# A block of gated linear attention, gated DeltaNet and MLP: the turned keys stored in whole rows, their 32x32 blocks put in place by GpSimd's loads

## The chip, the cores and the metric

The kernel runs on one core of a Trainium2 chip. The metric is the device time of one execution in microseconds (us). Runs of one kernel are summed up by their median; a profiled execution gives, besides its own time, a trace of every instruction and transfer. Engine names are short in the profile: PE is TensorE's matmul, PEld its weight load, DVE is VectorE, ACT is ScalarE, POOL is GpSimd, and SP is the engine that does nothing here but issue transfers. "SPq", "ACTq" and "POOLq" are the issues of transfers from these engines.

## What is computed

One layer over 1024 tokens of width 1024. After a norm with a modulation from a conditioning vector, one wide projection `w_in` gives the inputs of two branches: gated linear attention (GLA, 4 heads) and a gated delta rule (GDN, 8 heads). Their outputs are merged under sigmoid gates, projected by `w_out` and added to the input; a squared-ReLU MLP follows. The part that the change touches is the gated delta rule, cut here to what matters:

```python
k = l2_norm(silu(causal_short_conv(h @ w_in[keys])))        # 8 heads of 128 channels
def step(state, inp):                                        # over the chunks of 64 tokens
    qd, at, uu, ww, ks, dc = inp
    v_new = uu - einsum('bhcd,bhdv->bhcv', ww, state)
    o = einsum('bhcd,bhdv->bhcv', qd, state) + einsum('bhij,bhjv->bhiv', at, v_new)
    state = dc[..., None, None] * state + einsum('bhcd,bhcv->bhdv', ks, v_new)
```

The last product, keys times new values, sums over tokens, so it needs the keys with the token on the partitions. The projection leaves them the other way, with the channel on the partitions.

## The kernel before

All matmuls are float32 split into a high and a low half, three products each, on tiles of 128 x 512. The kernel is written as one stream of dense tiles. `dense_b` (line 477) makes one tile of 128 output channels by 1024 tokens in 8 steps, and each step ends in `tick()` (line 384). All other work is put on an agenda in ticks with `at` (line 373) and is emitted between the dense matmuls when its tick comes. `next_w` (line 472) fetches and casts the weights of the tile after the next: a block of 256 columns is loaded by SP into one of two buffers `raw`, ACT casts it to the high half `wH`, DVE subtracts for the low half `wL`.

The order on an engine is set by `InOrder` (from line 28). While it is strict, each instruction of that engine is issued after the one emitted before it. It is strict for PE, DVE, ACT, POOL and the queue `DMA` (SP) from the start until the second tile of `branch_gate` (lines 139 and 1507 to 1510). In the GDN heads it is strict again for PE, DVE and ACT only, and for POOL and SP from head 7 on (line 1870); until then the build orders POOL's and SP's queues as it expects their items to become ready. `ST` (line 68) is ACT's queue without `InOrder`.

Three stages matter here.

*Key phase.* The key tiles of the 8 heads are made one after another. `key_head` (line 749) schedules the rest of a head: the keys are stored as they are (`kT_d`), DVE turns them in 32x32 blocks into `kb` (`turn`), ACT squares `kb`, PE makes the Gram products, DVE multiplies them with the decays (`times`, line 786), and `spill` stores the result (`X_d`, `a21_d`). `V.transpose` turns each 32x32 block in its place, so each block is turned but the blocks stand where they were: the block of channels c and tokens (t, b) lies in row group c at columns (t, b), and has to come to row group b, columns (t, c). In the kernel before this is done on the way out: `spread` (lines 759 to 763) issues four stores, one for each 32 partitions of `kb`, in pieces of 32 floats (128 bytes), 1024 pieces a store, so that `kt_d[h]` holds the keys in their final order.

*Gates.* `branch_gate` (line 1392) makes 8 tiles with the `C_MA` columns of `w_in`. ACT applies tanh to a tile (`sig`) and stores it through `ST` to `sg_d`, 4 ticks later (line 1396).

*GDN heads.* `gdn_head` (line 919) runs 24 ticks of dense tiles for each head. At line 1025 one load brings `kt_d[h]` into `ktok`, a tile of the pool `hd` with 4 buffers, two of them in each head; PE uses it from tick 26 on (`c2`, line 1066). Heads 0 to 4 finish late: 62 ticks after their start POOL stores a row of norms (`on_d`, in `roots`), at tick 66 it loads that row broadcast to all partitions (`rows`), and at tick 72 DVE multiplies by it (`times`). That falls into the head after the next. In between POOL has nothing to do.

Of the kernel before, what the change touches and what calls it, by code (L numbers as in the profile page):

```python
# [50 lines left out]
def block_kernel(ctx: ExitStack, tc: tile.TileContext, x, c, ada_w, ada_b, pre_mix_w, post_mix_w,  # L51
# [15 lines left out]
    V, A, G, T = engines = [InOrder(tc, e) for e in (nc.vector, nc.scalar, nc.gpsimd, nc.tensor)]  # L67
    DMA, ST = InOrder(tc, nc.sync), nc.scalar
# [8 lines left out]
    def t4(shape=(128, 1024), dt=F32, p="t", tag="w4"):  # L77
        return w4.tile(list(shape), dt, tag=tag, name=nm(p), bufs=tag_bufs[tag])
# [4 lines left out]
    def pat(shape=(128, 512)):  # L83
        return pa.tile(list(shape), F32, tag="pa", name=nm("pa"))
# [288 lines left out]
    def at(dt, fn):  # L373
        agenda.append((clock[0] + dt, len(agenda) + uid[0] * 100000, fn))
        agenda.sort(key=lambda e: e[:2])
        uid[0] += 1
# [301 lines left out]
    kt_d = [dr.tile([128, 1024], F32, name=f"kt_d{h}") for h in range(8)]  # L678
# [22 lines left out]
    def r3(t, n=8):  # L701
        return t.rearrange("p (t q) -> p t q", t=n)
# [38 lines left out]
    def load_decay(h):  # L741
        Dk[h] = t4(p="gr", tag="hd")
        G.dma_start(Dk[h], gc_d[h].partition_broadcast(128))

    def mask_decay(h):
        G.affine_select(out=r3(Dk[h]), in_=r3(Dk[h]), compare_op=ALU.is_ge, fill=-1e30, base=0,
                        pattern=[[0, 8], [1, 128]], channel_multiplier=-1)

    def key_head(h, k, on, tr, sq, ex, gram, times_):

        z = {}

        def turn(hf):
            if not hf:
                z["kb"] = t4(p="ktok")
            h_ = slice(hf * 512, (hf + 1) * 512)
            V.transpose(z["kb"][:, h_], k[:, h_])

        def spread():

            dst = kt_d[h].rearrange("(b i) (t c j) -> c i t b j", i=32, t=8, j=32)
            for c_ in range(4):
                DMA.dma_start(dst[c_], z["kb"][32 * c_:32 * c_ + 32].rearrange("i (t b j) -> i t b j", t=8, j=32))

        def squares():
            z["kj"] = t4(p="kj")
            A.activation(z["kj"], z["kb"], AF.Square)

        def sums(hf):
            o = h * 32 + hf * 16  # L770
            V.reduce_sum(ssr[0][:, o:o + 16], r3(z["kj"][:, hf * 512:(hf + 1) * 512], 16), axis=mybir.AxisListType.X)

        def decays(hf):

            gr = Dk[h]
            for t in range(hf * 4, hf * 4 + 4):
                A.activation(gr[:, t * 128:(t + 1) * 128], gr[:, t * 128:(t + 1) * 128], AF.Exp,
                             bias=gcN[:, h * 8 + t:h * 8 + t + 1])

        def grams(hf):  # L780
            z["g", hf] = pt = pat()
            for i in range(4):
                kk = k[:, (hf * 4 + i) * 128:(hf * 4 + i + 1) * 128]
                T.matmul(pt[:, i * 128:(i + 1) * 128], kk, kk, start=True, stop=True)

        def times(hf):
            if not hf:
                z["a0"] = t4(p="a0")
            h_ = slice(hf * 512, (hf + 1) * 512)
            V.tensor_mul(z["a0"][:, h_], z.pop(("g", hf)), Dk[h][:, h_])  # L790

        def spill():
            Dk.pop(h)
            a3 = r3(z["a0"])
            xv = X_d[h * 16:(h + 1) * 16].rearrange("(t e) j i -> e j t i", e=2)
            DMA.dma_start(xv[0], a3[0:64, :, 0:64])
            DMA.dma_start(xv[1], a3[64:128, :, 64:128])
            DMA.dma_start(a21_d[h], a3[0:64, :, 64:128])

        on(tr[0], lambda: DMA.dma_start(kT_d[h], k))  # L800
        for hf in range(2):
            on(tr[hf], lambda hf=hf: turn(hf))
            on(sq[1] + 1 + hf, lambda hf=hf: sums(hf))
            on(ex[hf], lambda hf=hf: decays(hf))
            on(gram[hf], lambda hf=hf: grams(hf))
            on(times_[hf], lambda hf=hf: times(hf))
        on(sq[1], squares)
        on(tr[1] + 1, spread)
        on(ex[1] + 1, lambda: DMA.dma_start(Dt_d[h], Dk[h]))
        on(times_[1] + 1, spill)  # L810
        if h > 3:
            on(ex[0] - 8, lambda: load_decay(h))
            on(ex[0] - 3, lambda: mask_decay(h))
# [105 lines left out]
    def gdn_head(h, then=None):  # L919
# [3 lines left out]
        def on(t, fn):  # L923
            at(begin + t - clock[0], fn)
# [64 lines left out]
        z, turned = {}, h < 5  # L989
# [32 lines left out]
            on(33, columns)  # L1022

        ktok, eg = t4(p="kt", tag="hd"), t4(p="eg")
        DMA.dma_start(ktok, kt_d[h])
        DMA.dma_start(eg, gc_d[h].partition_broadcast(128))

        ke = t4(p="ke")
# [16 lines left out]
        c = {"st": None}  # L1045
# [429 lines left out]
    def on(t, fn):  # L1475
        at(begin + t - clock[0], fn)
# [4 lines left out]
    on(2, lambda: z1.__setitem__("t", key_tanh(keys[1])))  # L1481
    on(3, lambda: key_silu(keys[1], z1["t"]))
    key_head(0, keys[0], on, (2, 4), (3, 5), (19, 21), (21, 22), (22, 23))
    key_head(1, keys[1], on, (6, 10), (7, 11), (23, 23), (23, 23), (24, 24))
    for h, ps in enumerate(dense_n(6, h_rhs), 2):
        e_ = clock[0] - begin
        y, z_ = key_copy(h, ps), {}
        for s_ in (1, 2, 3):
            on(e_ + s_, lambda h=h, ps=ps, y=y, s_=s_: key_tap(h, ps, y, s_))
        on(e_ + 4, lambda y=y, z_=z_: z_.__setitem__("t", key_tanh(y)))  # L1490
        on(e_ + 5, lambda y=y, z_=z_: key_silu(y, z_["t"]))
        ends = {2: ((27, 29), (29, 30), (30, 31)), 3: ((31, 31), (31, 31), (32, 32))}.get(
            h, ((e_ + 11, e_ + 13), (e_ + 13, e_ + 14), (e_ + 14, e_ + 15)))
        key_head(h, y, on, (e_ + 9, e_ + 13), (e_ + 10, e_ + 14), *ends)
# [372 lines left out]
    for h in range(8):  # L1867
        if h == 7:
            for e in (G, DMA):
                e.last, e.strict = e.recent, True  # L1870
            stage0[0] = clock[0] + 24
            early = gla_plan()
            plan_ops(ga, 0, [e for e in early if e[0] < -8])
        gdn_head(h, (lambda: plan_ops(ga, 0, [e for e in early if e[0] >= -8])) if h == 7 else None)
# [566 lines left out]
    for n in range(len(seq)):  # L2441
        gi, key, c = seq[n]
# [106 lines left out]
```

## Time and profile before

| | before |
|---|---|
| median of 3 runs | 1891.47 us (1891.18 to 1894.53) |
| profiled execution, its own time | 1891.85 us |
| span from first to last instruction | 1890.1 us |
| granted TensorE clock, mean | 0.995 |
| `kt_d<-ktok` on SP | 32 stores of 128 KB, first 77.0, last 188.7 us |
| `kt<-kt_d` on SP | 8 loads of 512 KB, first 555.6, last 899.1 us |
| GpSimd's queue | 14336 packets, 22.44 MB |

The page of the profile gives the busy time of each engine and its share of the span. Below that, the span is cut into 40 equal slices of about 47 us, and each digit is a busy share in tenths; the row PEclk is the clock that TensorE was granted. Groups of instructions carry the names of the tiles they write and read, with buffer numbers left out, such as `kt_d<-ktok`. Lines of a group have the form "name, shapes, count | busy us, mean ns of one | idle time before them and what ended it". A line of the timeline has start, duration, engine, source line, operation and tiles; a bracket at its end is the idle time just before it, with the instruction that ended it. Nearly all instructions are recorded under line 38, that of the helper in `InOrder`, so the tiles tell them apart. A wait is put down to the release that came last.

### The profile page before, as it was taken

Reading aid. Unit: us, or ns where it says so; the run is one execution under the profiler, and the core shown is the slowest. Engines: PE = TensorE matmul, PEld = TensorE weight load, DVE = VectorE, ACT = ScalarE, POOL = GpSimd, SP = SyncE. Lnnn points to the kernel's source line nnn. Section 1 sums busy time; section 2 is a strip of 40 time slices with the busy share of each in tenths; the row PEclk is TensorE's granted clock in tenths of the full one; section 3 lists DMA queues with packets and bytes.
Section 4 is the critical chain, followed back from the end, with each engine's and each line's share of the span. In section 5 each row is a group of like instructions: output and inputs, shape, how many; then the busy total and the mean of one; then the engine's idle time right before and its main releaser. Section 6 shows DMA issues by size and latency. Waiting matters only on the chain. (4 is left out here: it accounts for less than half of the span.)

```text
span 1890.1 us, 26139 instructions
## 1 busy us (share of the span) xinstructions
PE 1850.0 (98%) x10057; PEld 1552.2 (82%) x10057; DVE 1415.7 (75%) x2201; ACT 866.3 (46%) x1393; POOL 152.9 (8%) x148
## 2 busy tenths in 40 slices
PE   7996999999999999999999999999999999999998
PEld 5785889889898888888888888878888888888886
DVE  6783754869676577778788778986788877777887
ACT  5453234352432444444654555568644446433333
POOL 2120010110101000000101010000022220000001
PEclk9998999999999999999999999999999999999999
DMA  9685673122234444454869566256667668262425
GB/s 321 205 235 149 187 178 103 58 87 86 74 100 149 122 133 144 144 149 123 265 186 245 184 172 187 74 172 224 220 205 235 232 215 319 68 223 106 162 101 101
DMA packets 285469, 313.80 MB, mean 166 GB/s; under 512 B 105922, under 2 KB 211856, under 8 KB 285344
## 3 DMA queue, kind: packets, MB, share of 16 engines
q1 hardware_dynamic: 254736, 274.73, 45.5%
q0 software_dynamic: 14336, 22.44, 6.4%
q10 hardware_dynamic: 16272, 14.95, 2.4%
q8 instruction: 79, 1.29, 0.3%
q14 instruction: 46, 0.38, 0.1%
HBM read 231.67 MB, written 80.41 MB: 165 GB/s over the span
## 5 line engine op out<-in xcount | busy, mean ns | idle before, releaser
L38 PE MATMUL pm<-hH,wH 128*128 128x512 f32 x864 | 285.9, 412 | 14.6 <-ACT wH L38 14.6
L38 PE MATMUL pm<-hL,wH 128*128 128x512 f32 x864 | 269.3, 393 | 0.0
L38 PE MATMUL pm<-hH,wL 128*128 128x512 f32 x864 | 267.8, 391 | 0.0
L38 PE MATMUL pm<-oH,wB 128*128 128x512 f32 x672 | 214.7, 394 | 0.4 <-DMA wB<-in_w_branch_gla_dram 0.4
L38 PE MATMUL pa<-w,yH 128*128 128x512 f32 (+1 forms) x696 | 212.5, 387 | 0.0
L38 PEld LDWEIGHTS pm<-hH,wL 128*128 128x128 f32 x864 | 162.4, 188 | 36.5
L38 PEld LDWEIGHTS pm<-hL,wH 128*128 128x128 f32 x864 | 162.7, 188 | 35.9
L38 PEld LDWEIGHTS pm<-hH,wH 128*128 128x128 f32 x864 | 146.3, 190 | 32.8 <-ACT wH L38 15.0
L38 DVE TENSOR_TENSOR w<-raw,w 128x512 fp32r<-128x512 f32 (+1 forms) x144 | 125.8, 876 | 40.9 <-ACT w L38 40.1
L38 PEld LDWEIGHTS pa<-w,yH 128*128 128x128 f32 x696 | 130.1, 188 | 26.9 <-DVE ya L38 0.4
L38 PEld LDWEIGHTS pm<-oH,wB 128*128 128x128 f32 x672 | 126.2, 188 | 26.6 <-DMA wB<-in_w_branch_gla_dram 0.9
L38 ACT CAST w<-raw 128x512 fp32r<-128x512 f32 (+1 forms) x144 | 99.4, 711 | 89.1 <-DVE raw L38 79.9
L38 PE MATMUL pa<-w,yL 128*128 128x512 f32 (+1 forms) x348 | 134.5, 387 | 0.0
L38 PE MATMUL pm<-oL,wB 128*128 128x512 f32 x336 | 130.8, 389 | 0.0
L38 PE MATMUL pa<-oB,w 128*128 128x512 f32 x480 | 111.9, 391 | 0.8 <-DVE oB L38 0.5
L38 DVE TENSOR_TENSOR wL<-raw,wH 128x1024 fp32r<-128x1024 f32 x62 | 75.6, 1222 | 48.5 <-ACT wH L38 48.4
L38 ACT CAST wH<-raw 128x1024 fp32r<-128x1024 f32 x62 | 64.4, 1045 | 91.4 <-DMA raw<-in_w_in_dram 34.5
L38 PEld LDWEIGHTS pa<-oB,w 128*128 128x128 f32 x480 | 89.6, 188 | 20.2 <-DVE oB L38 1.3
L38 DVE SCALAR_TENSOR_TENSOR cv<-pm,ccol,cv 128x1023 f32<-128x1023 f32 (+2 forms) x72 | 91.9, 1276 | 7.6 <-ACT cv L38 6.4
L38 PE MATMUL pm<-oT,w 128*128 128x512 f32 x384 | 90.8, 389 | 0.0
L38 PE MATMUL pa<-oT,w 128*128 128x512 f32 x384 | 90.8, 389 | 0.0
L38 DVE TENSOR_TENSOR ya<-pa,ya 128x512 f32<-128x512 f32 (+1 forms) x83 | 56.0, 683 | 43.7 <-PE pa L38 43.7
(425 smaller groups left out, 3702.2 us busy)
## 6 DMA issues: line engine op xcount, KB each, us to landing
yL<-y_d SPq DMA_DIRECT2D x53, 512.0 KB, 7.2
raw<-in_mlp_w_dram SPq DMA_DIRECT2D x23, 1024.0 KB, 6.1
raw<-in_w_in_dram SPq DMA_DIRECT2D x18, 1024.0 KB, 7.0
raw<-in_w_in_dram SPq DMA_DIRECT2D x32, 512.0 KB, 4.4
araw<-in_ada_w_dram SPq DMA_DIRECT2D x32, 512.0 KB, 4.0
raw<-in_mlp_w_dram SPq DMA_DIRECT2D x18, 512.0 KB, 5.3
araw<-in_ada_w_dram SPq DMA_DIRECT2D x32, 256.0 KB, 6.2
sl<-sg_d SPq DMA_DIRECT2D x16, 512.0 KB, 7.1
```

What stands on the lines that cost most here:

```text
L38: r = fn(*args, **kw)
```

## The change

The four stores of `spread` become one store of `kb` as it lies, in whole rows of 4 KB. `kt_d[h]` then holds the blocks in the wrong places. They are put in place when a GDN head loads them: the one load on SP becomes four loads on GpSimd's queue (`G`), each into 32 partitions of `ktok`, each in 1024 pieces of 32 floats.

```diff
@@ -756,12 +756,6 @@
-        def spread():
-
-            dst = kt_d[h].rearrange("(b i) (t c j) -> c i t b j", i=32, t=8, j=32)
-            for c_ in range(4):
-                DMA.dma_start(dst[c_], z["kb"][32 * c_:32 * c_ + 32].rearrange("i (t b j) -> i t b j", t=8, j=32))
@@ -805,7 +799,7 @@
         on(sq[1], squares)
-        on(tr[1] + 1, spread)
+        on(tr[1] + 1, lambda: DMA.dma_start(kt_d[h], z["kb"]))
         on(ex[1] + 1, lambda: DMA.dma_start(Dt_d[h], Dk[h]))
@@ -1022,7 +1016,9 @@
         ktok, eg = t4(p="kt", tag="hd"), t4(p="eg")
-        DMA.dma_start(ktok, kt_d[h])
+        src = kt_d[h].rearrange("(c i) (t b j) -> b i t c j", i=32, t=8, j=32)
+        for b_ in range(4):
+            G.dma_start(ktok[32 * b_:32 * b_ + 32].rearrange("i (t c j) -> i t c j", t=8, j=32), src[b_])
         DMA.dma_start(eg, gc_d[h].partition_broadcast(128))
```

## The prediction

> **What bounds the kernel now.** I read the page first: the engines' shares and the forty slices.
>
> ```profile
> span 1890.1 us, 26139 instructions
> PE 1850.0 (98%) x10057; PEld 1552.2 (82%) x10057; DVE 1415.7 (75%) x2201; ACT 866.3 (46%) x1393; POOL 152.9 (8%) x148
> PE   7996999999999999999999999999999999999998
> PEclk9998999999999999999999999999999999999999
> ```
>
> TensorE (PE) is busy for 1850.0 of 1890.1 us, so only its idle time, 40 us, can be won by anything that leaves its work alone, and the change does. The slices show where that idle time is: in the first slice (the start, which the change does not touch) and in the fourth, 142 to 189 us, with a busy share in the sixties and a clock below full. A change to the keys' way to DRAM lives in that fourth slice. Next I asked who waited for whom between 60 and 260 us.
>
> ```profile
> DVE wL L38 <- ACT wH L38: 37.6, 4, 25.3
> ACT wH L38 <- DMA raw<-in_w_in_dram: 30.9, 3, 23.1
> PE pm L38 <- ACT wH L38: 14.6, 1, 14.6
> ```
>
> Columns are total us, times, longest. It is one chain: a weight block of `w_in` lands late, ScalarE (ACT) stands 23.1 us until it can cast it, VectorE (DVE) 25.3 us behind the cast, and PE once, 14.6 us. The timeline of PE places it.
>
> ```profile
> 169.01 0.61 PE L38 MATMUL pm<-hH,wL 128*128 128x512 f32 x2
> 184.19 1.22 PE L38 MATMUL pm<-hH,wH 128*128 128x512 f32 x2 [14.56 <-ACT wH L38]
> 187.76 0.85 PE L38 MATMUL pm<-hL,wH 128*128 128x512 f32 x2
> 188.45 0.62 PE L38 MATMUL pm<-hH,wL 128*128 128x512 f32 x2
> 188.91 0.62 PE L38 MATMUL pm<-hH,wH 128*128 128x512 f32 x2
> ```
>
> PE stops after 169.6 and starts again at 184.19. It then runs five pairs of matmuls, to 188.45, in 4.26 us, where a pair at full pace takes 188.91 - 188.45 = 0.46 us: 2.0 us more are lost to the slow restart. The gap is worth 14.6 + 2.0 = 16.6 us.
>
> Why did the block land late? The timeline of the SP queue answers.
>
> ```profile
> 142.09 22.60 SPq L38 DMA_DIRECT2D kt_d<-ktok  x4
> 164.86 0.56 SPq L38 DMA_DIRECT2D Dt_d<-gr  x1
> 169.57 3.68 SPq L38 DMA_DIRECT2D kt_d<-ktok  x4
> 173.42 0.56 SPq L38 DMA_DIRECT2D Dt_d<-gr  x1
> 174.08 1.58 SPq L38 DMA_DIRECT2D X_d<-a  x2
> 176.43 0.64 SPq L38 DMA_DIRECT2D raw<-in_w_in_dram  x1
> ```
>
> The load is issued at 176.43, in a queue whose order is the program's. In front of it stand the four spread stores of head 5, stretched over 22.6 us, and the four of head 6. The waits of the SP queue from 141 to 170 us say what stretched them, and ACT's timeline shows the other end.
>
> ```profile
> SPq L38 <- DMA sg_d<-sig: 19.6, 1, 19.6
> 158.96 1.03 ACT L38 ACTIVATE sig<-pm 128x1024 f32<-128x1024 f32 x1 [2.02 <-DVE ssr L38]
> 160.01 0.34 ACTq L1396 DMA_DIRECT2D sg_d<-sig  x1
> 183.09 1.04 ACT L38 CAST wH<-raw 128x1024 fp32r<-128x1024 f32 x1 [23.11 <-DMA raw<-in_w_in_dram]
> ```
>
> SP stood 19.6 us in the middle of head 5's stores until ACT's store `sg_d` had landed, which was issued only at 160.01. The two share no data. I read it as a shared completion counter: the build deals a few counters to SP's and ACT's transfers in turn, in the order in which it expects them, and it expected SP's many small stores to run so late that `sg_d` came ahead of them. The view shows the wait, not this reason.
>
> **The spread removed, in the key phase.** Each head issues one store where it issued four, 24 fewer in all. DVE's and ACT's work on the keys stays. With fewer stores in front, and none in 128-byte pieces, I expect the build to put SP's transfers ahead of `sg_d` again, so that the load is held by its data alone. The item ahead of it is the spill of head 6, which waits for DVE's second product, and after the load comes the cast.
>
> ```profile
> 157.57 0.68 DVE L38 TENSOR_TENSOR a<-pa,gr 128x512 f32<-128x512 f32 x1
> DMA to landing us min/median/max: 5.7/6.1/6.6
> ```
>
> (The second line is the view of the tile `raw` from 141 to 200 us.) The product ends at 158.25. The spill took from 174.08 to 176.43, 2.35 us, so the load goes at 160.6, lands by 167.2 at the 6.6 us maximum, and is cast by 168.2 with the 1.04 us of the cast's row. PE wants it at 169.6. The whole 16.6 us go, with 1.4 us to spare. What is late next is that same load: 2 us more on it would bring back 0.6 us of waiting. DVE, idle from 158 to 184 us beside it, comes no later than PE.
>
> **The loads moved to GpSimd (POOL), in the GDN heads.** SP loses one issue per head, POOL's queue gains four, each 1024 pieces of 128 bytes. Two things can go wrong: the keys come too late for PE, or POOL comes late to what it does now. For the first, these are the load of head 3 on SP with the item behind it, the uses in the stretch from 744 to 790 us, which opens with head 3, and two groups of transfers with their us to landing.
>
> ```profile
> 697.03 0.32 SPq L38 DMA_DIRECT2D kt<-kt_d  x1
> 699.78 0.38 SPq L38 DMA_DIRECT2D raw<-in_w_in_dram  x1
> L38 PE MATMUL pa<-vn,kt x12: 271/274/377, 753.1 to 784.8; 128*128 128x128 f32 x12
> kt_d<-ktok SPq DMA_DIRECT2D x32, 128.0 KB, 3.5
> wB<-in_w_branch_gla_dram POOLq DMA_DIRECT2D x4, 512.0 KB, 10.3
> ```
>
> The load has 56 us until PE needs it. No row shows a POOL load in 1024 pieces. The nearest by pieces is the spread store, 3.5 us to landing on SP; the longest on POOL is 10.3 us, an accumulating load in 512 pieces. Four of those end to end are 14 to 41 us, inside 56. I cost this at nothing; the cover is gone only above 14 us apiece. SP, rid of the load, comes to the weight block behind it up to 2.7 us earlier; no slice there has PE idle, so that is worth nothing too.
>
> For the second, POOL's groups and timeline, and DVE's timeline behind it.
>
> ```profile
> L38 POOL DMA_DIRECT2D wB<-in_w_branch_gla_dram x4 | 5.8, 1440 | 47.4 <-DVE attT L38 35.4 <-ACT wB L38 6.2 <-PE pa L38 5.8
> L38 POOL DMA_DIRECT2D wB<-in_w_in_dram x4 | 5.1, 1284 | 23.4 <-ACT wB L38 23.4
> L38 POOL DMA_DIRECT2D gr<-gc_d x8 | 4.4, 550 | 6.2 <-DMA gc_d<-s 4.4 <-DVE ktok L38 1.0 <-issue 0.7
> 688.44 0.57 POOL L38 DMA_DIRECT2D on_d<-sqt  x1 [114.32 <-DVE sqt L38]
> 699.58 0.58 POOL L38 DMA_DIRECT2D row<-on_d  x1 [10.56 <-PE pa L38]
> 705.18 1.23 DVE L38 TENSOR_TENSOR si<-si,row 128x1024 f32<-128x1024 f32 x1 [2.15 <-DMA row<-on_d]
> 708.60 0.69 DVE L38 SCALAR_TENSOR_TENSOR si<-si,pm 128x512 f32<-128x512 f32 x1 [2.18 <-ACT si L38]
> 754.79 0.69 DVE L38 SCALAR_TENSOR_TENSOR si<-si,pm 128x512 f32<-128x512 f32 x1 [3.76 <-ACT si L38]
> 802.27 0.69 DVE L38 SCALAR_TENSOR_TENSOR si<-si,pm 128x512 f32<-128x512 f32 x1 [3.81 <-ACT si L38]
> 848.45 0.69 DVE L38 SCALAR_TENSOR_TENSOR si<-si,pm 128x512 f32<-128x512 f32 x1 [2.99 <-ACT si L38]
> ```
>
> POOL has two duties here for heads 0 to 4: it stores `on_d` and loads `row`, and DVE already waits for `row` (2.15 us at 705.18). The keys of head 3 become loadable at 697.03, `row` of head 0 at 699.58: 2.55 us apart, so the four issues can stand in front of `row`, and so again for heads 4, 5 and 6. What one issue takes, no row shows: 0.55 us (128 pieces, plain) is the floor, 2.9 us (twice the 1.44 us of 512 accumulating pieces) the ceiling. I take 2.0, an estimate from the nearer row: what 512 pieces add to 128 in the 1284 ns group, 0.73 us, counted twice on 0.55. If all four stand in front, `row` is 8.0 - 2.55 = 5.5 us late; DVE then has 2.18, 3.76, 3.81 and 2.99 us, in which it waits for ACT anyway, so at most 3.3 + 1.7 + 1.7 + 2.5 = 9.2 us over four heads. If one or two do, the delay is within DVE's waits and costs nothing. At the floor even four (2.2 us) cost nothing. A gain has no place here, since PE does not wait for these keys today. Between 0 and 9 us I take 1, near the lower end, because only the later of the four issues would run past the 2.55 us.
>
> **Sum.** Against the profiled execution's own 1891.85 us, span 1890.1: 1891.85 - 16.6 + 1 = 1876.3. The median of the runs is 0.4 us below that execution: 1876 us.
>
> **Rivals.** *The wait stays with SP.* If the build still deals `sg_d` its counter far ahead of SP, SP stands until it has landed, about 162.7, and saves only small stores behind that: head 5's from 162.7 to 164.86 and head 6's from 169.57 to 173.42, 6.0 us, less one whole-row store at about 0.6. The load goes 5.4 us earlier and the gap falls to 9.2: 1891.85 - 5.4 = 1886.4. For it: nobody has touched ACT's store. Against it: the spread is the largest share of SP's pieces per head (4096 of 128 bytes).
>
> *POOL's issues are dear.* With all four in front of `row`, the loss per head is four issues less 2.55 less DVE's mean spare 3.2. It eats the 16.6 us when that is 4.1 us over four heads, at 2.5 us an issue. At the ceiling of 2.9 it is 5.9 us a head, 23.4 in all: 1898.7, slower. For it: the ceiling comes from a row of this engine. Against it: those rows accumulate, and the order must be the worst one. The Trainium skill, "SBUF — State Buffer", section "SBUF: two separate sides", gives a way to it: GpSimd cannot write its descriptors while VectorE runs a two-port copy, and a transfer of about 620 ns then takes about 3100; by that the four issues are 12.4 us and the loss an estimated 27 us. The trace does not bear it out so far: POOL's `gr` loads, issued with DVE at work, hold 550 ns over eight.
>
> *Nothing moves.* The load could be held by another item at the same time, its buffer or a product, with the gap as it is: 1891.5.
>
> **How the numbers follow.** The forecast has 0.70, the wait that stays 0.12, dear issues 0.12, nothing 0.06. The range takes the forecast with its bounds (no cost in the heads, 1875, less 2 us for the spread of the runs before, 1891.18 to 1894.53; 9 us of cost, 1884) and the first rival: 1873 to 1887. About 0.2%, 3.8 us, is what a measurement of this kernel can tell from no change, so faster means under 1887.7: forecast and nearly all of the first rival, 0.81. Same gets 0.07, slower 0.12.
>
> **What would show it.** Right: no PE wait over 2 us in 140 to 190 us, the load of `raw` issued near 160, SP without a wait for `sg_d` of many microseconds, PE's fourth slice at 9; in the heads, POOL's four issues at about 2 us and DVE's wait for `row` below 6 us. Wrong: the gap still there behind SP, POOL issues above 2.5 us with DVE's wait for `row` grown to match, or PE waiting for `kt`.

## The result and the profile after

The changed kernel takes 1875.92 us (median of 6 runs, 1875.71 to 1877.93), the kernel before 1892.9 us beside it (1891.18 to 1894.53): a ratio of 0.9913, 95% interval 0.99 to 0.9926. The profiled execution took 1876.45 us, its span is 1874.7 us, against 1891.85 and 1890.1 before.

The page of the changed kernel: engine shares, the slices of PE and its clock.

```profile
span 1874.7 us, 26150 instructions
PE 1848.5 (99%) x10057; PEld 1550.6 (83%) x10057; DVE 1413.6 (75%) x2201; ACT 865.8 (46%) x1393; POOL 186.4 (10%) x180
PE   7999999999999999999999999999999999999998
PEclk9999999999999999999999999999999999999999
```

TensorE does the same 10057 matmuls in the same busy time (1848.5 us, 1850.0 before); its idle time fell from 40 to 26 us. The 6 in PE's fourth slice is now a 9, and so is the 8 in the row of its clock. The waits from 60 to 260 us, to be held against the three lines of the prediction (us in total, times, longest):

```profile
DVE wL L38 <- ACT wH L38: 19.6, 5, 11.3
ACT wH L38 <- DMA raw<-in_w_in_dram: 9.7, 2, 9.4
PE pa L38 <- DVE ssr L38: 0.7, 1, 0.7
```

The line of PE behind `wH` (14.6 us) is gone. ACT still waits for `raw`, but 9.4 us instead of 23.1, and PE does not notice. The SP queue over the same place, then ACT:

```profile
153.44 0.33 SPq L38 DMA_DIRECT2D kt_d<-ktok  x1
...
157.41 1.27 SPq L38 DMA_DIRECT2D X_d<-a  x2
158.73 0.64 SPq L38 DMA_DIRECT2D a_d<-a  x1
159.41 1.07 SPq L38 DMA_DIRECT2D raw<-in_w_in_dram  x1
```

```profile
157.76 1.03 ACT L38 ACTIVATE sig<-pm 128x1024 f32<-128x1024 f32 x1 [1.69 <-PE pm L38]
158.82 0.39 ACTq L1392 DMA_DIRECT2D sg_d<-sig  x1
168.19 1.05 ACT L38 CAST wH<-raw 128x1024 fp32r<-128x1024 f32 x1 [9.40 <-DMA raw<-in_w_in_dram]
```

Nothing in SP's queue waits for `sg_d` any more. The load goes at 159.41 instead of 176.43, directly behind head 6's spill, and the cast is done at 169.24. PE's timeline:

```profile
169.80 0.62 PE L38 MATMUL pm<-hH,wL 128*128 128x512 f32 x2
170.25 0.61 PE L38 MATMUL pm<-hH,wH 128*128 128x512 f32 x2
...
172.97 0.61 PE L38 MATMUL pm<-hH,wH 128*128 128x512 f32 x2
173.43 0.61 PE L38 MATMUL pm<-hL,wH 128*128 128x512 f32 x2
174.77 0.70 PE L38 MATMUL pa<-ssr,quad 128*128 128x256 f32 x2 [0.73 <-DVE ssr L38]
```

170.25 is the tile that started at 184.19 before, now without a wait and at full pace. In the GDN heads, POOL's timeline around heads 3 and 4, and PE's waits from 600 to 990 us:

```profile
682.49 0.99 POOL L38 DMA_DIRECT2D kt<-kt_d  x1 [8.36 <-PE pa L38]
684.79 0.59 POOL L38 DMA_DIRECT2D row<-on_d  x1 [1.32 <-PE pa L38]
686.23 2.94 POOL L38 DMA_DIRECT2D kt<-kt_d  x3 [0.85 <-issue]
...
728.66 0.98 POOL L38 DMA_DIRECT2D kt<-kt_d  x1 [8.37 <-PE pa L38]
730.61 0.58 POOL L38 DMA_DIRECT2D row<-on_d  x1 [0.97 <-PE pa L38]
731.17 2.97 POOL L38 DMA_DIRECT2D kt<-kt_d  x3
```

```profile
PE pa L38 <- DVE st L38: 0.7, 2, 0.5
PE pa L38 <- ACT rs L38: 0.5, 1, 0.5
```

In heads 3 to 6 one of the four loads stands ahead of `row`, three behind it; in head 7 all four are behind. PE waits 1.2 us in all over these heads, as before (1.5), and never for `kt`.

### The profile page after: what moved, and what is told of

Its sections match the earlier page's. It is cut to its first block, busy times and chain, and to the rows that moved or that the text cites. A ratio compares the mean times of both kernels' runs of the same rounds, so it can differ in the third digit from the quotient of the medians.

```text
span 1874.7 us, 26150 instructions
## 1 busy us (share of the span) xinstructions
PE 1848.5 (99%) x10057; PEld 1550.6 (83%) x10057; DVE 1413.6 (75%) x2201; ACT 865.8 (46%) x1393; POOL 186.4 (10%) x180
## 5 line engine op out<-in xcount | busy, mean ns | idle before, releaser
L38 PEld LDWEIGHTS pm<-oH,wB 128*128 128x128 f32 x672 | 126.2, 188 | 25.8 <-DMA wB<-in_w_branch_gla_dram 0.2
```

The costliest lines, as they stand in the source:

```text
L38: r = fn(*args, **kw)
```

## The experiments

The theory: each transfer counts up a completion counter when it has landed; the build has only a few of them for SP's and ACT's transfers and deals them in turn, and a transfer waits until the one that had its counter before has landed. SP stood because one of its stores had to take the counter that ACT's `sg_d` held; the order in which counters are dealt decides the stand, not the small pieces. The main rival: the stores in 128-byte pieces, by traffic or by their number, hold SP. All times beside the kernel before on the same chip:

| kernel | median us (runs) | before | ratio, 95% interval | PE behind `wH`, 100 to 200 us |
|---|---|---|---|---|
| changed kernel | 1875.92 (6) | 1892.9 | 0.9913 [0.99, 0.9926] | none |
| before, `sg_d` stored by GpSimd | 1880.3 (5) | 1893.98 | 0.9928 [0.9915, 0.994] | none |
| changed, block loads on SP | 1877.93 (4) | 1893.98 | 0.9915 [0.9901, 0.9928] | none |
| before, load on GpSimd | 1894.61 (11) | 1893.98 | 1.0003 [0.9994, 1.0012] | 14.6 |
| changed, four row stores | 1883.91 (5) | 1893.98 | 0.995 [0.9937, 0.9964] | 6.0 |
| before, one store halved | 1896.03 (1) | 1893.09 | one run | 16.3 |
| changed, late `row` | 1907.12 (5) | 1893.09 | 1.007 [1.0058, 1.0083] | none |
| changed, sixteen loads | 1884.59 (4) | 1893.09 | 0.9957 [0.9942, 0.9972] | none |

**The spread kept, `sg_d` taken off ACT's queue.**

```diff
-            at(4, lambda s_=s_, j=j: ST.dma_start(sig_d[0][j // 2][j % 2], s_))
+            at(4, lambda s_=s_, j=j: G.dma_start(sig_d[0][j // 2][j % 2], s_))
```

> The kernel before with one edit: the first gate branch's stores `sg_d` are issued by GpSimd instead of ScalarE, so they share no completion counter with SP's stores; the four spread stores stay. My theory (SP's 19.6 us stand is a wait on a shared completion counter): SP no longer stands behind `sg_d`, the load of `raw` goes between 160 and 166 us instead of 176.43, TensorE's gap of 14.6 us shrinks to 0 to 4 us, and the time is 1876 to 1881 us, though all 32 stores in 128-byte pieces are still there. Rival (the small pieces themselves, as traffic or as number of issues, hold SP): SP still needs until about 176 us, the gap stays 12 to 15 us, and the time is 1889 to 1893.

SP's queue in this kernel:

```profile
143.81 4.33 SPq L38 DMA_DIRECT2D kt_d<-ktok  x4
...
154.50 3.08 SPq L38 DMA_DIRECT2D kt_d<-ktok  x4
...
160.77 0.64 SPq L38 DMA_DIRECT2D raw<-in_w_in_dram  x1
```

Head 5's four small-piece stores take 4.33 us instead of 22.60 and head 6's 3.08; the load goes at 160.77. The gain is nearly all there with every 128-byte piece in place, so the rival falls. Against the changed kernel some 3 us are missing by the ratios (0.9928 beside 0.9913) and 4.4 us by the medians; the two intervals overlap. In the profile 1.5 us of it come at 940 to 950 us, far from this place.

**The store alone, and the load alone.**

```diff
 changed kernel, store alone:
-            G.dma_start(ktok[32 * b_:32 * b_ + 32].rearrange("i (t c j) -> i t c j", t=8, j=32), src[b_])
+            DMA.dma_start(ktok[32 * b_:32 * b_ + 32].rearrange("i (t c j) -> i t c j", t=8, j=32), src[b_])
 kernel before, load alone:
-        DMA.dma_start(ktok, kt_d[h])
+        G.dma_start(ktok, kt_d[h])
```

> The changed kernel with the four block loads of each GDN head issued by SP instead of GpSimd: the whole-row store alone. My theory: all of the gain belongs to the store, so the time is within 2 us of the changed kernel (1874 to 1878). Rival (SP's four issues of 1024 pieces hold back the weight blocks behind them in the heads, so the move to GpSimd is worth something of its own): new TensorE waits behind `wH` or `wL` between 550 and 900 us, and the time is 1880 or more.

> The kernel before with its one whole-row load of the keys per GDN head issued by GpSimd, the spread stores kept: the move of the load alone. My theory: nothing waits for that load on either queue, so the time is that of before, 1890 to 1894, with the gap at 184 us as it was. Rival (SP freed of the load reaches its weight blocks earlier and gains in the heads): 1885 or less.

The store alone gives the whole gain (0.9915 beside 0.9913), the load alone nothing (1.0003). The latter's SP queue and PE show the stand and the gap unmoved:

```profile
143.85 21.60 SPq L38 DMA_DIRECT2D kt_d<-ktok  x4
```

```profile
184.97 1.22 PE L38 MATMUL pm<-hH,wH 128*128 128x512 f32 x2 [14.60 <-ACT wH L38]
```

That GpSimd issues the loads is worth nothing that these runs can tell: with the loads on SP, PE waits 3.2 us instead of 1.2 from 600 to 990 us.

**Whole rows, but four stores.**

```diff
-        on(tr[1] + 1, lambda: DMA.dma_start(kt_d[h], z["kb"]))
+        on(tr[1] + 1, lambda: [DMA.dma_start(kt_d[h][32 * c_:32 * c_ + 32], z["kb"][32 * c_:32 * c_ + 32]) for c_ in range(4)])
```

> The changed kernel with its one whole-row store split into four, of 32 partitions each and still in rows of 4 KB: as many issues as before, but no 128-byte pieces. My theory (shared counter): as the program is now built, `sg_d` of the first gate tile shares its counter with the store `a21_d` of head 5, so SP stands there until `sg_d` has landed, near 162.6 us; about eleven issues at 0.65 us follow, the load of `raw` goes near 169.5, lands near 176 to 178, and TensorE has a gap of 7 to 10 us: 1883 to 1887 us. Rival (the traffic of the small pieces was the cause, and that is gone): no stand, gap 0 to 2 us, 1875 to 1878. Second rival (only the count of issues matters, each at its 0.6 us): SP without a stand, `raw` near 168, gap 5 to 7 us.

SP's queue, its waits from 120 to 200 us, and PE:

```profile
144.32 1.27 SPq L38 DMA_DIRECT2D X_d<-a  x2
161.09 0.52 SPq L38 DMA_DIRECT2D a_d<-a  x1
...
168.36 0.64 SPq L38 DMA_DIRECT2D raw<-in_w_in_dram  x1
```

```profile
SPq L38 <- DMA sg_d<-sig: 17.4, 2, 15.5
```

```profile
175.99 1.22 PE L38 MATMUL pm<-hH,wH 128*128 128x512 f32 x2 [5.97 <-ACT wH L38]
```

The stand is back, 15.5 us long, without any small piece, and at another item: after head 5's `X_d`, ahead of `a_d` (that is `a21_d`), as the expectation had it from the counters of the built program. PE's wait is 1 us shorter than the 7 to 10 us expected, and the time (1883.91 us) lies in the interval expected. The second rival had named the same place for the load (near 168) and the same gap (5 to 7 us), so these two do not tell it from the theory; but it had SP without a stand, and SP stood.

**One more store in front.**

```diff
 spread of the kernel before:
+                if h == 4 and c_ == 3:
+                    for i_ in (0, 16):
+                        DMA.dma_start(dst[c_][i_:i_ + 16], z["kb"][96 + i_:112 + i_].rearrange("i (t b j) -> i t b j", t=8, j=32))
+                    continue
```

> The kernel before with head 4's last spread store split in two halves of 16 partitions: one more transfer in SP's queue between head 4 and `sg_d`, so every later transfer of SP takes the next completion counter. My theory (shared counter, dealt in turn): SP stands behind `sg_d` for the same 19 to 20 us, but one store earlier, at head 5's first store instead of its second; `raw` goes at 176 to 178 us, the time is 1890 to 1895. Rival (the stand comes from the stores' own traffic or from the place of the item in the program): it stays at the second store.

```profile
144.61 0.66 SPq L38 DMA_DIRECT2D kT_d<-cv  x1
162.78 2.79 SPq L38 DMA_DIRECT2D kt_d<-ktok  x4
...
177.04 0.64 SPq L38 DMA_DIRECT2D raw<-in_w_in_dram  x1
```

Its waits from 120 to 200 us:

```profile
SPq L38 <- DMA sg_d<-sig: 18.2, 2, 17.4
```

Before, the stand lay inside head 5's four stores (142.09, 22.60 us for the four). Here all four follow it, in 2.79 us: it has moved one store forward, which is what a counter dealt in turn makes of one more transfer. It is 17.4 us rather than 19 to 20, and ends with the landing of `sg_d` (issued at 160.09, landed 2.6 us later; SP goes on at 162.78); the load goes as late as before. The time, one run, is 1 us above the interval expected.

**The price of a late `row`.** Nothing is left out; the memsets are overwritten by the load.

```diff
             c["row"] = t4(p="row")
+            for _ in range(8):
+                G.memset(c["row"], 0.0)
```

> The changed kernel with eight memsets of the `row` tile put on GpSimd ahead of the load that overwrites it, in heads 0 to 4: 0.95 us each by the 947 ns of the `U` memsets, 7.6 us. All four block loads then stand in front of `row` as well, so `row` comes 7 to 9 us later: the price of dear issues, without the issues being dear. By my prediction's way of counting (what exceeds VectorE's 2.2 to 3.8 us of waiting for ScalarE is lost to the end): VectorE's wait for `row` grows to 8 to 11 us a head, 4 to 6 us a head are lost, 20 to 29 us in all, 1896 to 1905 us. Rival (VectorE has more room behind `row` than that, and TensorE does not follow it): VectorE waits as long, but TensorE's waits between 600 and 990 us grow by less than 5 us in all, and the time is 1875 to 1881.

DVE's waits and PE's, 600 to 990 us:

```profile
DVE si L38 <- DMA row<-on_d: 46.3, 5, 11.5
DVE si L38 <- ACT si L38: 12.6, 3, 5.6
```

```profile
PE pa L38 <- ACT vn L38: 15.8, 4, 4.5
PE pa L38 <- DVE ob L38: 3.4, 1, 3.4
```

DVE's wait for `row` grows by 42.7 us (3.6 in the changed kernel) and its wait for ACT falls by 13.2 (25.8 there): 29.5 us net, by the prediction's way of counting, and the kernel is 31.2 us above the changed one, 2 us more than the 20 to 29 expected. In part that is a larger dose: counted from its `on_d`, `row` is issued 8.1 to 11.0 us later than in the changed kernel, where 7 to 9 were expected. PE's own waits are 19 us of the loss, the rest goes with the slow restart after each (mean granted clock 0.95 from 640 to 930 us, 1.00 in the changed kernel). So the rival "dear issues" priced a late `row` rightly to within some 2 us, and lacked only the dear issues.

**Sixteen loads a head.**

```diff
-            G.dma_start(ktok[32 * b_:32 * b_ + 32].rearrange("i (t c j) -> i t c j", t=8, j=32), src[b_])
+            for i_ in (0, 8, 16, 24):
+                G.dma_start(ktok[32 * b_ + i_:32 * b_ + i_ + 8].rearrange("i (t c j) -> i t c j", t=8, j=32), src[b_][i_:i_ + 8])
```

> The changed kernel with each of the four block loads cut into four (8 partitions, 256 pieces each): sixteen issues a head on GpSimd, the same pieces. If an issue costs by its pieces, one takes a quarter of the 0.78 us at which the 1024-piece loads followed one another plus little, 0.25 to 0.4 us, and the sixteen 4 to 6 us; if it costs by the issue, 0.6 to 0.8 us each and 10 to 13 us for sixteen. My theory of the time: nothing waits for these loads, TensorE has 40 us and more of cover, 1875 to 1879 either way. Rival: the load of `row` or the keys come late, VectorE's wait for `row` or a TensorE wait for `kt` shows, 1880 or more.

POOL's timeline, then DVE's waits (600 to 990 us) and the landing of ACT's stores `od_d` (560 to 930 us; in the changed kernel 2.8/4.3/6.7):

```profile
730.86 0.59 POOL L38 DMA_DIRECT2D row<-on_d  x1 [1.18 <-PE pa L38]
731.43 6.13 POOL L38 DMA_DIRECT2D kt<-kt_d  x8
738.30 0.73 POOL L38 DMA_DIRECT2D kt<-kt_d  x1 [0.73 <-DMA kt<-kt_d]
```

```profile
DVE sqt L38 <- DMA od_d<-si: 10.8, 4, 3.4
```

```profile
DMA to landing us min/median/max: 5.1/7.0/10.2
```

My theory of the time fell: 8.7 us are lost, and neither by `row` nor by `kt`. The loads now run on beside `od_d`, which lands 2.7 us later in the median; DVE has to wait for it before it writes `sqt` (10.8 us, 0.7 in the changed kernel), and PE follows. That chain is read from the trace and was not tested by a run of its own. Back to back, the issues of 256 pieces start 0.65 us apart, those of 1024 pieces in the changed kernel 0.77 us: a load costs POOL by the issue far more than by the piece.

## Why the prediction was right

*The gap.* From the last pair before it (169.01 before, 169.80 after) to the seventh pair of the next tile (188.91 and 172.97) the changed kernel saves 16.7 us; 16.6 were expected, wait and slow restart together.

*The load of `raw`.* Expected to go at 160.6, it went at 159.41. It was to land in at most 6.6 us and took 8.8 (ACT takes it up at 168.19). The two misses nearly cancel: the cast ends at 169.24, and 1.0 us is to spare where 1.4 was expected.

*What is late next.* Here a step failed: "DVE, idle from 158 to 184 us beside it, comes no later than PE." DVE's order is fixed, so it too stood until the cast (`wL` at 169.27), and its sums `ssr` come late to PE by the 0.73 us at 174.77. DVE after, then DVE and PE before:

```profile
169.27 1.23 DVE L38 TENSOR_TENSOR wL<-raw,wH 128x1024 fp32r<-128x1024 f32 x1 [11.30 <-ACT wH L38]
174.04 0.68 DVE L38 TENSOR_REDUCE ssr<-kj 128x16 f32<-128x512 f32 x1
```

```profile
188.93 0.67 DVE L38 TENSOR_REDUCE ssr<-kj 128x16 f32<-128x512 f32 x1
189.84 0.59 PE L38 MATMUL pa<-ssr,quad 128*128 128x256 f32 x2
```

Before, PE's slow restart had hidden that: the sums were done at 189.60, and PE came to them at 189.84. Counted from the same last pair ahead of the gap, 15.9 us are saved by that matmul, and 15.4 by the 1200th, after one more such wait (0.2 us, for DVE's `nbrC`).

*POOL in the heads.* 1 us was allowed, at 2.0 us an issue with all four ahead of `row`. In heads 3 to 6 one stands ahead, the four take 3.9 us, DVE's wait for `row` is 3.6 us (4.1 before) and the cost is nothing. The Trainium skill, "SBUF — State Buffer", section "SBUF: two separate sides", says that GpSimd's descriptors starve while VectorE copies over two ports. The 3.1 us there is the time of a whole transfer, and the prediction took it for GpSimd's issue. No issue here came to that: the longest of 28 between 560 and 930 us took 1.6 us with DVE busy for 74% of that stretch, the longest of the 122 with sixteen loads a head 2.2 us. Whether a two-port copy ran beside any of them, the traces do not say.

*The sum.* So 16.7 - 1.3 + 0 = 15.4 us against 16.6 - 1 = 15.6 expected. The last pair ahead of the gap itself came 0.8 us later in the changed kernel, and as much was won back further on; neither is in the sum or explained. The closeness of 1876.45 to 1876.3 owes something to two terms of 1 us, one missed and one not needed.

*The reason.* The shared counter was only inferred in the prediction, and no trace shows the counters themselves. The runs bear it out in three ways: the stand goes when `sg_d` leaves ACT's queue, it moves by one transfer when one transfer is put in, and it comes back elsewhere when whole rows go out in four stores. The halved store also says when the counter was dealt. In a deal in turn, had both halves been dealt theirs ahead of `sg_d`, `sg_d` would have moved on with the stores behind it, and the stand would have stayed where it was. So `sg_d` got its counter ahead of the last of them, which SP had issued by 141.3 us, while `sg_d` itself went at 160.09: the build did expect SP to be later than it was, as the prediction read it. For a better order the prediction gave two grounds, fewer stores and none in 128-byte pieces. Four row stores meet the second alone, and SP stood again, so small pieces gone are not enough. What the change did right is therefore partly luck of the count: "whole rows" without "one store" gives back 7 to 8 us, by the first rival's mechanism, at another item. The Trainium skill, "DMA: Bandwidth & Descriptors", section "Why a DMA increments its semaphore by 16 and not by 1", advises one counter for each transfer in flight, because a shared count can be reached too early. The trace shows the other face of it: a shared one that is kept safe costs a wait, here 15.5 to 19.6 us on a transfer that had no data in common with its holder.

## What to carry to other kernels

When a queue stands behind a transfer with which it shares no data, suspect a shared counter: it can be tested by moving that one transfer to another queue, or by adding one in front. Any change in the number of transfers can reshuffle who waits for whom, so look again at every queue after it. And when a gap is closed, ask which engine had been resting in its shadow: it sets the next wait.

## What the runs showed of the hardware

- GpSimd's issue of 1024 pieces of 128 bytes took 0.96 to 1.6 us each, four in 3.9 us, since they overlap; of 256 pieces 0.73 us at the least; a plain `row` load of 128 pieces 0.59 us.
- With sixteen loads a head GpSimd waited 17 times for one of its own earlier loads to land (15.0 us in all from 560 to 930 us; 738.30 above is one), with four never. In heads 3 to 6 the first such wait came each time behind a row of eight loads (731.43 above).
- The same pieces leave other marks on the two queues (queue, kind: packets, MB, share of the 16 DMA engines), in the changed kernel and with the loads on SP:

```profile
q1 hardware_dynamic: 221456, 270.54, 45.0%
q0 software_dynamic: 15872, 26.64, 7.4%
```

```profile
q1 hardware_dynamic: 254736, 274.73, 46.0%
q0 software_dynamic: 14336, 22.44, 6.6%
```

On SP the 32 loads are 33280 packets, on GpSimd 1536. The engines' time is about the same, 1.0% and 0.8% of the span.
